# Four DMAs at the head of a bf16 batched matmul: the first a and b loaded in another order

## Chip, core and metric

The kernel runs on one core of a Trainium2 chip, alone on it. The metric is device time in microseconds, the median of repeated executions. One further execution was profiled; its trace gives the time of every instruction and every DMA packet.

## The reference

```python
def reference(a, b):          # a: (16, 512, 512) = (batch, k, m), b: (16, 512, 512) = (batch, k, n), float32
    return np.matmul(a.transpose(0, 2, 1), b).astype(np.float32)
```

Sixteen independent products of 512x512 matrices, with a stored k-first. 33.55 MB are read and 16.78 MB are written, all in float32; the kernel converts to bf16 on the chip and multiplies there.

## The kernel before

**Pairs.** The 16 batches are taken two at a time, so there are eight pairs. A pair's a, and its b, is one SBUF tile of 128 partitions x 8 rows x 512 floats (16 KB in each partition, 2 MB in all). In pairs 1 to 7 the 64 lower partitions hold one batch and the 64 upper ones the other, and one DMA of 2 MB fills the tile. Four such tiles, x0 to x3, are used in turn: a of pair 0 is in x0, b in x1, a of pair 1 in x2, and so on.

**Pair 0 is cut finer.** Its two batches are loaded one after the other, each over all 128 partitions with four rows per partition, so that work can begin after 1 MB of a and 1 MB of b. Batch 0 is cut once more. Of its 512 rows of k, the first 128 go one to a partition (256 KB, one run of 2 KB per partition: `top_v`), and the other 384 go three to a partition (768 KB, one run of 6 KB per partition: `low_v`). Both pieces of a count on one semaphore, `s_f[0]`, both pieces of b on `s_f[1]`; the conversion waits for the full count of 32. Batch 1 of pair 0 follows with one DMA of 1 MB for a and one for b (line 77).

**Engines.** All DMAs are issued by SyncE (SP in the profile) in the order of the program, and all stand in one hardware queue, `q1`, which feeds 16 DMA engines. A load puts eight packets of data on each of the 16 (one per partition) and a four-byte completion packet after them. SP's order is: the four pieces of batch 0 (lines 74 and 75), batch 1 of pair 0 (line 77), fourteen whole tiles (line 83; the last b is cut in two, lines 85 and 86), then the outputs (line 91), the last of them at line 192. From the third pair's a on, a load waits at line 80 until the tile that it overwrites has been converted; the marker for that is the one-element memset of line 102 or 123, which raises `s_in`. The outputs wait for `s_h`, the first half of the last b, at line 88, and for ScalarE's marker `s_out` at line 90: no output is sent before nearly all loads are through.

VectorE (DVE) converts float32 to bf16: lines 98 (pair 0) and 117 (the others), 128x2048 elements at a time. TensorE (PE) multiplies (lines 135 and 155), ScalarE (ACT) copies PSUM to the output tiles (lines 174 and 180). In pair 0 VectorE converts a of batch 0, then b of batch 0, each as soon as its `s_f` is complete; TensorE starts once both are done (line 129).

Of the kernel before, what the change touches and what calls it, by code (L numbers as in the profile page):

```python
# [8 lines left out]
def kernel(  # L9
# [62 lines left out]
    with tc.tile_critical(no_gpsimd_drain=True):  # L72
        for j in range(2):
            nc.sync.dma_start(x_ts[j][:, 0:1, :], top_v[j]).then_inc(s_f[j], 16)  # L74
            nc.sync.dma_start(x_ts[j][:, 1:RV, :], low_v[j]).then_inc(s_f[j], 16)  # L75
        for j in range(2):
            nc.sync.dma_start(x_ts[j][:, RV:R, :], in0_v[j][1]).then_inc(s_x[j], 16)  # L77
# [145 lines left out]
```

## Time and profile before

| | |
|---|---|
| median of 15 runs | 123.64 us (123.28 to 123.96) |
| the profiled execution | 123.85 us, of which 122.1 us are the span from the first to the last instruction |
| DMA packets in the span | 5200, 50.33 MB, 97.6% of 16 engines' time, mean 412 GB/s |
| TensorE matmul / VectorE / ScalarE busy | 62.0 / 38.1 / 32.1 us |
| packets by size | 464 of 4 B, 256 of 2 KB, 256 of 6 KB, 2560 of 8 KB, 1664 of 16 KB |
| typical time of one packet | 84 ns (2 KB), 234 ns (6 KB), 309 ns (8 KB), 611 ns (16 KB) |
| issue of the four pieces of batch 0 | 0.94, 1.39, 1.86 and 2.32 us after the start of the span, each taking 0.39 to 0.43 us of SP |
| from issue to landing of the four | 2.8 us (a, 256 KB), 4.3 us (a, 768 KB), 4.5 us (b, 256 KB), 6.6 us (b, 768 KB) |

The page shares out the span by engine, and the chain of waits says what ended last. A stretch view gives, for a window of time, each engine's busy time and two DMA columns: the share of 16 DMA engines' time, and GB/s. A packet is counted there in the window in which it starts, so in short windows the share can be above 1: packets that began there took longer than the window. The sizes and times of single packets are in the packet records that the trace keeps.

### The profile page before, as it was taken

To read this page: it belongs to the slowest core of one execution; us is meant where nothing else is said; L and a number is where in the kernel's file an instruction comes from. 1 tells how busy PE (TensorE), PEld (TensorE's weight loads), DVE (VectorE), ACT (ScalarE), POOL (GpSimd) and SP (SyncE) were. 2 spreads that over 40 slices of the span, in tenths; PEclk is the share of its full clock that TensorE was granted. 3 is DMA by queue.
4 is the path that set the end of the run, shared out by engine and by line. 5 is a ranking of instruction groups with operands and counts; after the bars stand their busy time and mean duration, and the time that the engine had idled before them with its cause. 6 is when DMAs were issued, how large, how long until landed. Compare 5 with 4: busy or idle time off the path is not lost.

```text
span 122.1 us, 1209 instructions
## 1 busy us (share of the span) xinstructions
PE 62.0 (51%) x480; PEld 35.0 (29%) x480; DVE 38.1 (31%) x48; ACT 32.1 (26%) x41; POOL 0.2 (0%) x4
## 2 busy tenths in 40 slices
PE   0005928379969749979919928989900000000000
PEld 0002404035446324636606605656500000000000
DVE  0133070681394092474356437492000000000000
ACT  4000332400560840091470290091570000000000
POOL 0000000000000000000000000000000000000000
PEclk9999999959999985999999999999997555555555
DMA  3999999999999999999999999999999999999993
GB/s 80 390 419 427 456 435 429 435 435 435 429 429 429 429 429 429 429 429 429 429 429 429 429 429 416 421 427 427 429 429 429 429 427 429 429 429 424 421 427 142
DMA packets 5200, 50.33 MB, mean 412 GB/s; under 512 B 464, under 2 KB 464, under 8 KB 976
## 3 DMA queue, kind: packets, MB, share of 16 engines
q1 hardware_dynamic: 5200, 50.33, 97.6%
HBM read 33.55 MB, written 16.78 MB: 412 GB/s over the span
## 4 chain that ended last, share of the span: by engine, by line
DMA 59%; DVE 6%; issue 3%; ACT 3%; SPq 3%; ACTq 0%
DMA x<-in_b_dram 53%; DMA out_dram<-o 6%; ACT o L180 3%; DVE bbf L117 3%; DVE abf L117 3%; SPq L77 1%; SPq L75 1%; SPq L74 1%; SPq L83 0%; DVE done L123 0%; ACTq L72 0%; SPq L218 0%; SPq L72 0%
## 5 line engine op out<-in xcount | busy, mean ns | idle before, releaser
L155 PE MATMUL ps<-bbf,abf 64*128 64x512 bf16 x448 | 52.9, 393 | 13.2 <-PEq L150 13.2
L155 PEld LDWEIGHTS ps<-bbf,abf 64*128 64x128 bf16 x448 | 31.2, 112 | 34.8 <-issue 20.2
L180 ACT COPY o<-ps 128x1024 f32<-128x1024 f32 x28 | 26.3, 1027 | 40.6 <-PE ps L155 36.5
L117 DVE CAST abf<-x 128x2048 bf16<-128x2048 f32 x14 | 17.1, 1224 | 17.3 <-PE ps L155 13.3
L117 DVE CAST bbf<-x 128x2048 bf16<-128x2048 f32 x14 | 17.2, 1225 | 14.3 <-DMA x<-in_b_dram 14.2
L135 PE MATMUL ps<-bbf,abf 128*128 128x512 bf16 x32 | 9.1, 448 | 13.2 <-PEq L133 13.2
L135 PEld LDWEIGHTS ps<-bbf,abf 128*128 128x128 bf16 x32 | 3.7, 122 | 18.1 <-issue 16.1
L174 ACT COPY o<-ps 128x1024 f32<-128x1024 f32 x4 | 4.1, 1014 | 17.1 <-PE ps L135 17.1
L98 DVE CAST abf<-x 128x2048 bf16<-128x2048 f32 x2 | 2.5, 1226 | 11.5 <-PE ps L135 5.8
L98 DVE CAST bbf<-x 128x2048 bf16<-128x2048 f32 x2 | 2.4, 1224 | 2.0 <-DMA x<-in_b_dram 2.0
L185 ACT ACTIVATE done<-done 1x1 uint32<-1x1 uint32 x8 | 1.6, 197 | 0.0
L174 ACT ACT_TABLE_LOAD x1 | 1.3, 1283 | 0.9 <-SPq L72 0.9
L123 DVE MEMSET done<- 1x1 f32 x14 | 0.8, 59 | 0.0
L102 DVE MEMSET done<- 1x1 f32 x2 | 0.1, 59 | 0.0
L207 POOL MEMSET const-bfloat16-1.0<- 128x1 bf16 x1 | 0.1, 101 | 0.0
L207 POOL MEMSET const-uint8-127<- 128x1 uint8 x1 | 0.1, 101 | 0.0
L207 POOL MEMSET const-float32-0.0<- 128x1 f32 x1 | 0.1, 98 | 0.2 <-issue 0.2
L207 POOL MEMSET const-float32-1.0<- 128x1 f32 x1 | 0.1, 98 | 0.0
## 6 DMA issues: line engine op xcount, KB each, us to landing
out_dram<-o SPq DMA_DIRECT2D x8, 2048.0 KB, 21.8
x<-in_a_dram SPq DMA_DIRECT2D x7, 2048.0 KB, 12.1
x<-in_b_dram SPq DMA_DIRECT2D x6, 2048.0 KB, 15.9
x<-in_b_dram SPq DMA_DIRECT2D x3, 1024.0 KB, 13.5
x<-in_a_dram SPq DMA_DIRECT2D x1, 1024.0 KB, 8.6
x<-in_a_dram SPq DMA_DIRECT2D x1, 768.0 KB, 4.3
x<-in_b_dram SPq DMA_DIRECT2D x1, 768.0 KB, 6.6
x<-in_a_dram SPq DMA_DIRECT2D x1, 256.0 KB, 2.8
```

The lines of the kernel that those rows point to most:

```text
L74: nc.sync.dma_start(x_ts[j][:, 0:1, :], top_v[j]).then_inc(s_f[j], 16)
L75: nc.sync.dma_start(x_ts[j][:, 1:RV, :], low_v[j]).then_inc(s_f[j], 16)
L77: nc.sync.dma_start(x_ts[j][:, RV:R, :], in0_v[j][1]).then_inc(s_x[j], 16)
L98: nc.vector.tensor_copy(out=bf_ts[0][:], in_=x_ts[j][:, u * RV:(u + 1) * RV, :]).then_inc(s_cast, 1)
L117: nc.vector.tensor_copy(out=(bbf_ts if n % 2 else abf_ts)[v][:], in_=x_ts[n % NX][:, v * RV:(v + 1) * RV, :],).then_inc(s_cast, 1)
L123: nc.vector.memset(dve_done[:, n:n + 1], 0.0).then_inc(s_in, 1)
L135: mm = nc.tensor.matmul(ps_ts[0][h][:, t % 2, :], a_m[:, r, t], bbf_ts[0][:, r, :], start=(r == 0), stop=(r == RV - 1),)
L155: mm = nc.tensor.matmul(ps_ts[g][h][:, t % 2, :], a_m[:, t], bbf_ts[v][rows, r, :], start=(v == 0 and r == 0), stop=(v == V - 1 and r == R ...
L174: nc.scalar.copy(out=o_ts[0][:, g, 2 * h:2 * h + 2, :], in_=ps_ts[0][h][:]).then_inc(s_ev[h], 1)
L180: ev = nc.scalar.copy(out=o_ts[i % NO][:, g, 2 * h:2 * h + 2, :], in_=ps_ts[g][h][:])
L185: nc.scalar.memzero(act_done[:, i:i + 1]).then_inc(s_out, 1)
L207: nc = _bacc.Bacc("TRN2", target_bir_lowering=False, num_devices=1)
```

## The change

The four issues of batch 0 come in another order: a's 2 KB runs, b's 2 KB runs, a's 6 KB runs, b's 6 KB runs. Sources, destinations, sizes, semaphores and all waits are the same; no other instruction moves. One line is added to the program, so every line below it has a number higher by one in the kernel after.

```diff
     with tc.tile_critical(no_gpsimd_drain=True):
         for j in range(2):
             nc.sync.dma_start(x_ts[j][:, 0:1, :], top_v[j]).then_inc(s_f[j], 16)
+        for j in range(2):
             nc.sync.dma_start(x_ts[j][:, 1:RV, :], low_v[j]).then_inc(s_f[j], 16)
         for j in range(2):
             nc.sync.dma_start(x_ts[j][:, RV:R, :], in0_v[j][1]).then_inc(s_x[j], 16)
```

## Prediction

> **What bounds the kernel now.** I read the page's second and third parts first.
>
> ```profile
> DMA  3999999999999999999999999999999999999993
> GB/s 80 390 419 427 456 435 429 435 435 435 429 429 429 429 429 429 429 429 429 429 429 429 429 429 416 421 427 427 429 429 429 429 427 429 429 429 424 421 427 142
> q1 hardware_dynamic: 5200, 50.33, 97.6%
> ```
>
> The 16 DMA engines are full from the first slice to the last; TensorE, the busiest compute engine, has 51%. The time is one stream of 50.33 MB plus what stands before and behind it. An instruction in pair 0 matters only if it opens a gap in that stream, or makes one engine later than the rest. So I looked at both ends of the stream with the stretch view (its last two columns: share of the DMA engines, GB/s).
>
> ```profile
> 0.90:1.80 0.90, 0.00 (x0) 0.00 (x0) 0.00 (x0) 0.90 (x1) 0.00 (x0) 1.00 0.00 0
> 1.80:2.40 0.60, 0.00 (x0) 0.00 (x0) 0.00 (x0) 0.38 (x1) 0.00 (x0) 1.00 1.00 109
> 2.40:3.00 0.60, 0.00 (x0) 0.00 (x0) 0.00 (x0) 0.00 (x0) 0.00 (x0) 1.00 0.65 253
> 3.40:5.00 1.60, 0.00 (x0) 0.00 (x0) 0.00 (x0) 0.00 (x0) 0.00 (x0) 1.00 1.02 419
> 5.40:5.60 0.20, 0.00 (x0) 0.00 (x0) 0.00 (x0) 0.00 (x0) 0.00 (x0) 1.00 1.08 389
> 5.60:5.90 0.30, 0.00 (x0) 0.00 (x0) 0.21 (x1) 0.00 (x0) 0.00 (x0) 1.00 1.83 499
> 5.90:8.60 2.70, 0.00 (x0) 0.00 (x0) 1.01 (x1) 0.00 (x0) 0.00 (x0) 1.00 0.96 402
> 119.90:120.30 0.40, 0.00 (x0) 0.00 (x0) 0.00 (x0) 0.00 (x0) 0.00 (x0) 0.50 0.36 144
> 120.30:120.90 0.60, 0.00 (x0) 0.00 (x0) 0.00 (x0) 0.00 (x0) 0.00 (x0) 0.50 0.07 27
> ```
>
> Data start about 1.96 us (packet records), 1.0 us after the first issue. By 3.00 us 0.6 x 109 + 0.6 x 253 = 217 KB are through, so a's 256 KB end near 3.1. The row 5.40:5.60 holds 2 KB packets alone: 389 GB/s, so a 256 KB piece is 262 KB / 389 = 0.67 us. The row 3.40:5.00 holds 6 KB packets: 419 GB/s, so a 768 KB piece is 786 KB / 419 = 1.88 us.
>
> Two rows matter more than the rates. In 5.60:5.90, where b's 6 KB runs begin, 499 x 0.3 = 150 KB were started; at 26.2 GB/s per engine (419 / 16) that is 5.7 engine-us of work, but 1.83 x 0.3 x 16 = 8.8 were recorded: some 3 engine-us of stall. The packet records give its shape: two 6 KB packets took 1.09 us in place of 0.234, five took 0.45 to 0.52. At the other such place, a's first 6 KB runs at about 3.05, eight packets took 0.39 to 0.64. Then the end: in 120.30:120.90 the share is 0.07, and 27 x 0.6 = 16 KB, two packets of 8 KB. So two engines finish about half a microsecond after the other fourteen. A stall of 0.86 us on two engines at 5.9 us can live to the end, because each engine has its own fixed share of every transfer and never idles; completion packets fit this, since in the later transfers two of 16 always land some 0.5 us late.
>
> The ends add up: 1.96 us to the first byte, 118.85 of stream (to 120.81), 1.30 to the end of the span, 1.75 outside it (123.85 less 122.1). The median, 123.64, is 0.21 below this execution; I make the sum against 123.85 and carry the difference to the median.
>
> VectorE's rows show the cover on the compute side, SP's the issues:
>
> ```profile
> 0.94 0.39 SPq L74 DMA_DIRECT2D x<-in_a_dram  x1
> 1.39 0.42 SPq L75 DMA_DIRECT2D x<-in_a_dram  x1
> 1.86 0.42 SPq L74 DMA_DIRECT2D x<-in_b_dram  x1
> 2.32 0.43 SPq L75 DMA_DIRECT2D x<-in_b_dram  x1
> 5.68 1.23 DVE L98 CAST abf<-x 128x2048 bf16<-128x2048 f32 x1 [5.68 <-DMA x<-in_a_dram]
> 8.95 1.23 DVE L98 CAST bbf<-x 128x2048 bf16<-128x2048 f32 x1 [2.04 <-DMA x<-in_b_dram]
> ```
>
> **What the skill says.** The Trainium skill, "DMA: Bandwidth & Descriptors", section "Queues, rings and completion order": each DMA engine consumes one queue's descriptors in ring order. The trace agrees: 6 KB packets begin only when the 2 KB ones are through. Its section "Where 436 GB/s comes from" puts the fabric's ceiling at 435 GB/s; the page's long plateau is 429. "HBM Reference", section "Latency", gives an HBM access 0.2 us on average and 2 us under high load: the stalls of 0.16 to 0.86 us lie in that span, though the trace doesn't show that they are read latency.
>
> **The change part by part.** Nothing is removed or added. a's 768 KB issue moves behind b's 256 KB issue on SP: it starts at 1.86 in place of 1.39, b's small one at 1.39 in place of 1.86. Each still takes 0.39 to 0.43 us of SP, and everything from 2.32 on keeps its time.
>
> *Does the queue run dry?* First data came 1.0 us after issue, so the second transfer is ready at 2.4 and needed at 3.1 (0.7 spare); a's large one is ready at 2.9 and needed at 3.1 + 0.67 = 3.8 (0.9 spare); b's large one is ready at 3.3 and needed at 3.8 + 1.88 = 5.7. Cost 0. Were that cover gone, the gap would go straight into the time.
>
> *When do the tiles land?* a gets b's 256 KB ahead of it: its conversion moves from 5.68 to 6.35 and ends at 7.58. Behind it on VectorE is b's conversion, which waits for data until 8.95, with the same bytes ahead of it as before; 1.37 us spare, so TensorE still starts at 10.5. Cost 0. Even a TensorE start later by a microsecond would be harmless: the first load that waits for VectorE is issued at 17.29, while the loads ahead of it land only at 23.6 (the last of them was issued at 4.29 and took 19.3 us).
>
> *What happens to the stalls?* This is the only term that can show. Both groups stood at a change from 2 KB to 6 KB packets; at 6 to 8 KB there is none above 0.05 us, at 6 to 2 KB one of 0.17. Before there are two such changes; after there is one, and one place where a 2 KB transfer follows a 2 KB transfer, which the trace of before doesn't contain. Lower bound: the long stalls don't occur, the two late engines end with the rest, -0.5 us. Upper bound: a second stall of the long kind on an engine that has one already, +0.86. I take 0: a stall follows each short transfer (0.67 us gives little time to fetch what comes next), and there are two short transfers in either order.
>
> Sum: 123.85 + 0 + 0 + 0, carried to the median 123.64; I write 123.65. A difference under 0.2%, 0.25 us, is about what can't be told from no change.
>
> **The rivals.**
>
> *Slower: the stalls pile up.* After the change both exposed places lie back to back at 3.1 and 3.8 us, with no long transfer between them in which an engine's reads could run ahead again. If one engine has the 0.4 us kind at the first and the 0.86 kind at the second, and an engine decides the end that had only one before, the time is +0.3 to +0.6: 124.1. It decides when the slowest engine's stalls exceed 0.86 by 0.25. For it: eight of 16 engines stalled at the first place already. Against it: of the two engines with the long stall one seems to have had 0.30 at the first place too, and the other none, so the sum of both was partly there before.
>
> *Faster: the long stall is a matter of b's 6 KB runs following its 2 KB runs.* With a's 1.88 us between them it goes; the last two packets end with the rest, and 0.5 us is saved: 123.1. For it: the long stall stood there alone. Against it: a's large piece now starts after a 2 KB transfer and a full stream, just as b's did.
>
> *The change doesn't reach the time in any way but a conversion of a later by 0.67 us.* This is the forecast itself: the order of four pieces within the first 2 MB, hidden behind the wait for the second of them.
>
> **How the numbers follow.** Same 0.40 (123.65, own range 123.4 to 123.9), slower 0.36 (at 124.1, reaching 124.5 at the bound), faster 0.24 (at 123.1). I lean to slower over faster because two short transfers in a row are the one condition that is new, and a new exposed place costs more easily than it gives. The range that leaves about 2 in 10 outside is 123.1 to 124.25.
>
> **What would show it.** Right: issues in the new order at the same four times; a's first conversion near 6.35, b's near 8.95, TensorE at 10.5; stalled packets at about 3.1 and 3.8, none at 5.7; two packets alone at the end near 120.8. b's conversion at 8.4, and no lone packets at the end, would be the faster rival; b's conversion past 9.2 with every later load late by the same amount the slower one. The reasoning itself is wrong if the DMA share drops below full in 2.4 to 4 us (the queue ran dry), or if the time moves by more than the lateness of the slowest engine does.

## The result and the profile after

The kernel after takes 125.62 us (median of 9, 125.0 to 126.25) against 123.58 us for the kernel before on the same chips (median of 47). The ratio is 1.0163, 95% interval 1.0148 to 1.0178. The prediction was 123.65 us, no change, with a range of 123.1 to 124.25 us; the measured time lies above it.

The page of the kernel after, DMA rows of its second and third part:

```profile
DMA  2999999999999999999999999979999999999992
GB/s 69 375 405 423 454 427 422 438 427 427 380 396 448 427 443 427 427 427 433 422 427 448 427 438 409 419 309 406 422 435 427 435 427 427 422 422 435 425 438 108
q1 hardware_dynamic: 5200, 50.33, 96.0%
```

Same packets, same bytes, but 96.0% of the engines' time in place of 97.6%, in a span of 124.2 us in place of 122.1. The plateau is the same; there are dents at the start, in slices 11 and 12 (380 and 396 GB/s, from 31.0 to 37.3 us), and in slice 27 (309 GB/s). The span has grown by 2.1 us, and the profiled execution by as much (125.99 against 123.85).

The timeline of the kernel after (start, length, instruction; in brackets the idle time before and what ended it):

```profile
0.94 0.39 SPq L74 DMA_DIRECT2D x<-in_a_dram  x1
1.39 0.42 SPq L74 DMA_DIRECT2D x<-in_b_dram  x1
1.86 0.42 SPq L76 DMA_DIRECT2D x<-in_a_dram  x1
2.33 0.43 SPq L76 DMA_DIRECT2D x<-in_b_dram  x1
...
4.22 1.41 SPq L84 DMA_DIRECT2D x<-in_b_dram  x1
8.87 1.23 DVE L99 CAST abf<-x 128x2048 bf16<-128x2048 f32 x1 [8.87 <-DMA x<-in_a_dram]
10.72 1.23 DVE L99 CAST bbf<-x 128x2048 bf16<-128x2048 f32 x1 [0.62 <-DMA x<-in_b_dram]
```

The issues came in the new order at the foreseen times. a's conversion, foreseen at 6.35 us, starts at 8.87; b's, foreseen at 8.95, at 10.72. One issue, the eighth, held SP for 1.41 us in place of 0.45; the trace doesn't show why. The stretch view (last two columns: share of the 16 DMA engines, GB/s) shows what happened in between:

```profile
2.40:3.40 1.00, 0.00 (x0) 0.00 (x0) 0.00 (x0) 0.00 (x0) 0.00 (x0) 1.00 0.89 326
3.90:4.80 0.90, 0.00 (x0) 0.00 (x0) 0.00 (x0) 0.00 (x0) 0.00 (x0) 1.00 0.90 373
4.80:5.70 0.90, 0.00 (x0) 0.00 (x0) 0.00 (x0) 0.00 (x0) 0.00 (x0) 1.00 0.87 362
5.70:6.30 0.60, 0.00 (x0) 0.00 (x0) 0.00 (x0) 0.00 (x0) 0.00 (x0) 1.00 0.78 318
6.30:7.50 1.20, 0.00 (x0) 0.00 (x0) 0.00 (x0) 0.00 (x0) 0.00 (x0) 1.00 1.06 410
81.00:82.50 1.50, 1.50 (x18) 0.89 (x14) 1.41 (x2) 0.00 (x0) 0.00 (x0) 1.00 0.42 175
122.40:123.00 0.60, 0.00 (x0) 0.00 (x0) 0.00 (x0) 0.00 (x0) 0.00 (x0) 0.50 0.07 27
```

The same stretches of the kernel before, for comparison:

```profile
3.90:4.80 0.90, 0.00 (x0) 0.00 (x0) 0.00 (x0) 0.00 (x0) 0.00 (x0) 1.00 1.02 423
5.70:6.30 0.60, 0.00 (x0) 0.00 (x0) 0.60 (x1) 0.00 (x0) 0.00 (x0) 1.00 1.18 376
81.00:82.50 1.50, 1.36 (x14) 0.94 (x16) 1.50 (x3) 1.50 (x2) 0.00 (x0) 1.00 1.01 426
```

From 3.9 to 5.7 us a share of 0.87 to 0.90 is 14 of 16 engines. The packet records say the same: two engines had finished b's 2 KB runs at 3.9 us and got their first packet of a's 6 KB runs only at 6.3 to 6.5 us, at least 4.4 us after that transfer's issue. On the other engines it was there when it was needed, from 3.81 us on, so after 1.95 us or little more. Between 5.8 and 6.2 us two more engines stood still, at the change to the fourth transfer. Of the sixteen completions of a's 768 KB, fourteen come at 6.01 to 6.34 us and two at 8.68 and 8.84; a's conversion waits for all sixteen. The two stay behind: in 122.40:123.00 there are again two packets alone (27 x 0.6 = 16 KB).

How the 2.14 us between the two profiled executions (125.99 less 123.85) come together can be read from the last completion of one and the same transfer. For a's 1 MB of batch 1 it stands at 13.17 us, before at 11.38: 1.8 us later. In the kernel before, too, two engines were late by then, by some 0.6 us; the pair's longer hole makes most of the 1.8. First data at 2.32 us in place of 1.96 goes into the same sum, but in this execution alone: in the next profile of this kernel they come at 1.96, and the time is no shorter. The 1.8 us still stand at 30 us (30.21 against 28.42). By 50 us they have become 2.2 (50.03 against 47.87), and so they stay to the end.

The last 0.4 us come in at a later hole, between 32 and 36 us:

```profile
29.95 0.33 SPq L84 DMA_DIRECT2D x<-in_a_dram  x1
32.00:34.00 2.00, 2.00 (x22) 1.29 (x19) 1.23 (x1) 0.00 (x0) 0.00 (x0) 1.00 0.93 336
```

The same two in the kernel before:

```profile
26.00 0.33 SPq L83 DMA_DIRECT2D x<-in_a_dram  x1
32.00:34.00 2.00, 1.58 (x16) 0.65 (x12) 0.74 (x1) 2.00 (x3) 0.00 (x0) 1.00 1.05 451
```

With both conversions late, TensorE starts at 12.24 us in place of 10.48, takes 5.18 us for its second batch in place of 3.62, and VectorE reaches the next pair at 26.40 in place of 22.33. So this load, the eleventh transfer, is issued only at 29.95 us in place of 26.00. The first engines need it at 32.09. Three engines then stand still; their first packets come between 32.7 and 33.4 us, up to 3.5 us after the issue. The late pair has work there, but its packets, like the others', are longer while the stream recovers (up to 0.93 us in place of 0.61, at 34 to 35 us). That this hole is what costs the pair 0.4 us is read from the time alone: in the next profile, with the same load issued at 30.81 us, the last engines lose nothing there.

The row 81.00:82.50 is one more hole, in the other fourteen engines. SP waits at line 89 for the first half of the last b before it sends outputs, and that is complete only when the late pair is; the timely engines have nothing left by then.

### The profile page after: what moved, and what is told of

It is laid out like the page before. It is cut to its first block, busy times and chain, and to the rows that moved or that the text cites. A ratio compares the mean times of both kernels' runs of the same rounds, so it can differ in the third digit from the quotient of the medians.

```text
span 124.2 us, 1209 instructions
## 1 busy us (share of the span) xinstructions
PE 62.7 (50%) x480; PEld 35.0 (28%) x480; DVE 37.9 (30%) x48; ACT 32.1 (26%) x41; POOL 0.2 (0%) x4
## 2 busy tenths in 40 slices
DMA packets 5200, 50.33 MB, mean 405 GB/s; under 512 B 464, under 2 KB 464, under 8 KB 976
## 3 DMA queue, kind: packets, MB, share of 16 engines
q1 hardware_dynamic: 5200, 50.33, 96.0%
## 5 line engine op out<-in xcount | busy, mean ns | idle before, releaser
L156 PE MATMUL ps<-bbf,abf 64*128 64x512 bf16 x448 | 51.3, 385 | 14.4 <-PEq L151 14.4
L136 PE MATMUL ps<-bbf,abf 128*128 128x512 bf16 x32 | 11.4, 534 | 15.0 <-PEq L134 15.0
```

The source lines that it names most:

```text
L136: mm = nc.tensor.matmul(ps_ts[0][h][:, t % 2, :], a_m[:, r, t], bbf_ts[0][:, r, :], start=(r == 0), stop=(r == RV - 1),)
L156: mm = nc.tensor.matmul(ps_ts[g][h][:, t % 2, :], a_m[:, t], bbf_ts[v][rows, r, :], start=(v == 0 and r == 0), stop=(v == V - 1 and r == R ...
```

## Experiments

**Is it a fixture of each order?** Both kernels were profiled once more.

> The kernel before, profiled once more, to see whether the late pair of DMA engines is a fixture of this order. Theory P (the late pair sets the end, and it is made late in the first 8 us by a fixed cause): again a stall near 5.9 us on two engines, about 0.9 us each, again two completions of 16 that land some 0.5 us after the rest in every later transfer, time 123.3 to 123.9. Rival R (the stalls are chance): another number of engines, another place, or none.

123.68 us, in one execution. Of the kernel before again, stretch view:

```profile
3.90:4.80 0.90, 0.00 (x0) 0.00 (x0) 0.00 (x0) 0.00 (x0) 0.00 (x0) 1.00 1.05 437
4.80:5.70 0.90, 0.00 (x0) 0.00 (x0) 0.00 (x0) 0.00 (x0) 0.00 (x0) 1.00 0.91 357
5.70:6.30 0.60, 0.00 (x0) 0.00 (x0) 0.45 (x1) 0.00 (x0) 0.00 (x0) 1.00 1.00 341
```

This time four to five engines stood still between 5.8 and 6.3 us, where b's 6 KB runs, the fourth transfer, are due; the lateness is spread over more engines. At 3.9 to 4.8 us nearly all were busy (1.05). In these two executions the place is the same and the number of engines is not: theory P in its strict form (always a pair) fell.

> The kernel after, profiled once more. In its first profile two engines did nothing between 3.9 and 6.3 us: they had finished b's 2 KB runs and had no packet of a's 6 KB runs. Theory P: the same hole of 2.0 to 2.6 us on two engines, a's landing near 8.8 us, time 125 to 126.3. Rival R: the hole moves or is missing in this execution, and the time with it.

126.39 us, in one execution. Of the kernel after again:

```profile
3.90:4.80 0.90, 0.00 (x0) 0.00 (x0) 0.00 (x0) 0.00 (x0) 0.00 (x0) 1.00 0.81 253
4.80:5.70 0.90, 0.00 (x0) 0.00 (x0) 0.00 (x0) 0.00 (x0) 0.00 (x0) 1.00 0.72 266
5.70:6.30 0.60, 0.00 (x0) 0.00 (x0) 0.00 (x0) 0.00 (x0) 0.00 (x0) 1.00 0.90 297
```

253 GB/s in place of 423: eight engines stood still at 3.75 to 4.5 us, three of them past 6 us (their completions of a come at 9.3, the first at 6.0). In both profiles of this kernel the hole begins as soon as the second transfer is through; the number of engines and the width differ.

**Which of the two holes costs?**

```diff
-        nc.sync.wait_ge(s_h, 16)
         for i in range(pairs - 1):
             nc.sync.wait_ge(s_out, i + 1)
```

> The kernel after without SP's wait for the first half of the last b ahead of the outputs. After the change this wait let the 14 timely engines run dry from 81.0 to 82.6 us (0.86 us of 16 engines' time). Theory P (the end is set by the two late engines, which never run dry after 6.3 us): the gap closes, the 14 others end earlier, and the time stays at 125.6 within 0.3. Rival G (the loss is this gap): about 0.9 us comes back, 124.7.

125.19 us, ratio 1.0145 (1.0104 to 1.0186). Of this kernel:

```profile
3.90:4.80 0.90, 0.00 (x0) 0.00 (x0) 0.00 (x0) 0.00 (x0) 0.00 (x0) 1.00 0.45 137
...
81.00:82.50 1.50, 1.15 (x13) 0.52 (x10) 1.42 (x2) 1.50 (x3) 0.00 (x0) 1.00 1.00 421
```

The gap at 81 us is closed (421 GB/s), and 1.45% of the 1.63% remain. By these ratios a ninth of the loss is the wait ahead of the outputs; the intervals overlap and allow anything from nothing to a third. The time lies between the two forecasts, nearer to theory P's. Most of the loss is thus made earlier; in this execution ten engines stood still after 3.7 us.

**Do the later issues crowd out the third transfer?** The 256 KB pieces got semaphores of their own, `s_t`, VectorE waits for them as well, and SP waits before the fifth issue (only this line is shown, with the two lines behind it):

```diff
+        nc.sync.wait_ge(s_t[0], 16)
         for j in range(2):
             nc.sync.dma_start(x_ts[j][:, RV:R, :], in0_v[j][1]).then_inc(s_x[j], 16)
```

> The kernel after, with SP waiting for the landing of a's 256 KB (near 3.8 us) before it issues the fifth transfer and all later ones; the 256 KB pieces get semaphores of their own for that. Theory S (what the two engines lack is the third transfer's work, which reaches them late because the two transfers ahead of it are short; later issues have no part in it): the hole of 2.4 us stays, 125.6. Rival Q (the fifth to eighth issue, which crowd behind it between 2.8 and 5.6 us, hold it up): the hole shrinks below 1 us, and the time goes to 124.2 or less.

Median 125.99 us over 20 runs, 1.9% above the kernel before (123.64). They scatter from 123.43 to 126.90, and 18 of the 20 took 124.89 us or more. The ratio on record, 1.006 (1.0021 to 1.01), is drawn from the quickest few and says little here. The hole is there while only the fourth transfer stands behind the third: SP issues the fifth at 3.69 us, when the first engines are already running dry.

```profile
3.90:4.80 0.90, 0.00 (x0) 0.00 (x0) 0.00 (x0) 0.00 (x0) 0.00 (x0) 1.00 0.33 116
4.80:5.70 0.90, 0.00 (x0) 0.00 (x0) 0.00 (x0) 0.00 (x0) 0.00 (x0) 1.00 0.88 266
```

Rival Q is out: the hole did not shrink. Two of the runs came in at 123.4. That fits a delay that differs from execution to execution, with the third transfer sometimes in time; it isn't shown, as those two runs weren't profiled.

**How much must stand ahead of the third transfer?** Three forms, their first four issues made by SP at the same times. The lines that differ are shown, without the lines that they replace:

```diff
# whole: one DMA of 1 MB each, 8 KB runs
+            nc.sync.dma_start(x_ts[j][:, 0:RV, :], in0_v[j][0]).then_inc(s_f[j], 16)
# 4 KB runs: four pieces of 512 KB
+    top_v = [x[0][0:2 * P].rearrange("(p r) m -> p r m", r=2) for x in (a, b)]
# 6 KB first
         for j in range(2):
             nc.sync.dma_start(x_ts[j][:, 1:RV, :], low_v[j]).then_inc(s_f[j], 16)
         for j in range(2):
             nc.sync.dma_start(x_ts[j][:, 0:1, :], top_v[j]).then_inc(s_f[j], 16)
```

> a and b of batch 0 are each one DMA of 1 MB with 8 KB runs; no 256 KB pieces. Theory S (the third transfer's work reaches a DMA engine only some 3 to 4.5 us after its issue once the stream runs, at 4.8 to 6.3 us of the span, and an engine that is through with the first two transfers before that stands still): the third transfer is needed only at 2 + 2 x 2.5 = 7 us, so no engine stands still, no late engine at the end, 122.9 to 123.5, no slower than the kernel before. Rival K (two transfers of the same size in a row are what stalls, whatever the size): engines stand still near 4.5 or 7 us, 124.5 or more.

> The order of the kernel after, but each of the four pieces is 512 KB with 4 KB runs. Theory S: the third transfer is needed at about 2 + 2 x 1.25 + 0.3 = 4.8 us, in the midst of its arrival times of 4.8 to 6.3: fewer engines stand still, the last two or three of them up to 1.5 us in place of 2.4; the time lies between both kernels, 124.0 to 125.0. Rival P (only what follows a packet of 2 KB stalls): no engine stands still, 123.5 or less.

> The same four pieces with the two of 768 KB first: a's 6 KB runs, b's 6 KB runs, a's 2 KB runs, b's 2 KB runs. Theory S: the third is needed at 2 + 2 x 1.88 + 0.2 = 6.0 us, the fourth at 6.6, the fifth at 7.3: nearly all has arrived, no hole over 0.5 us, 123.2 to 123.8. Rival P (what follows 2 KB packets stalls): two short transfers in a row as in the kernel after, so engines stand still at 7.3 us, 125 or more.

| first two transfers | first engine through with both, us | measured, us | ratio to before (95%) |
|---|---|---|---|
| 2 x 256 KB (kernel after) | 3.8 | 125.62 | 1.0163 (1.0148 to 1.0178) |
| 2 x 512 KB (4 KB runs) | 4.9 | 124.05 (123.09 to 124.57) | 1.0022 (1.0000 to 1.0043) |
| 256 + 768 KB (kernel before) | 5.0 | 123.64 | 1 |
| 2 x 768 KB (6 KB first) | 6.3 | 123.48 | 0.9987 (0.9978 to 0.9995) |
| 2 x 1 MB (whole) | 7.4 | 123.21 (123.13 to 123.39) | 0.9963 (0.9951 to 0.9976) |

The medians fall with each step, though between 4 KB runs and the kernel before the interval reaches 1. The cleanest pair is the kernel after and 6 KB first: the same four pieces in another order, and 125.62 against 123.48 us. Three stretch views (4 KB runs, 6 KB first, whole, in this order):

```profile
4.80:5.70 0.90, 0.00 (x0) 0.00 (x0) 0.00 (x0) 0.00 (x0) 0.00 (x0) 1.00 0.98 319
```

```profile
4.80:5.70 0.90, 0.00 (x0) 0.00 (x0) 0.00 (x0) 0.00 (x0) 0.00 (x0) 1.00 0.96 389
5.70:6.30 0.60, 0.00 (x0) 0.00 (x0) 0.00 (x0) 0.00 (x0) 0.00 (x0) 1.00 1.07 451
6.30:7.50 1.20, 0.00 (x0) 0.00 (x0) 0.00 (x0) 0.00 (x0) 0.00 (x0) 1.00 0.98 379
```

```profile
4.80:5.70 0.90, 0.00 (x0) 0.00 (x0) 0.00 (x0) 0.00 (x0) 0.00 (x0) 1.00 1.00 419
5.70:6.30 0.60, 0.00 (x0) 0.00 (x0) 0.49 (x1) 0.00 (x0) 0.00 (x0) 1.00 1.00 423
6.30:7.50 1.20, 0.00 (x0) 0.00 (x0) 0.74 (x1) 0.00 (x0) 0.00 (x0) 1.00 1.02 430
```

With 4 KB runs there is still a dent, 319 GB/s; eleven completions of the third transfer come by 6.65 us, the other five 0.3 to 1.5 us later. With 6 KB first, two transfers of 2 KB packets in a row stand at 6.3 to 7.5 us and run at their usual rate. Rivals K and P are out: neither two equal transfers in a row nor what follows 2 KB packets stalls. The whole form beats both kernels: no engine is late at the end, and 0.43 us is saved. Not all of that is lateness. Summed over the packet records its packets took 1893 us of engine time, those of the kernel before 1903: 0.6 us less for each of 16 engines. In the 6 KB order a's conversion starts at 7.74 us, 2.06 later than before, at no cost; but b's, for which TensorE waits as well, starts at 8.88 (8.95 before). The cover that this shows is a's behind b's, and no more.

**Is it the time of the issue?**

```diff
-            nc.sync.dma_start(x_ts[j][:, 1:RV, :], low_v[j]).then_inc(s_f[j], 16)
+            nc.scalar.dma_start(x_ts[j][:, 1:RV, :], low_v[j]).then_inc(s_f[j], 16)
```

> The kernel after with the two 768 KB pieces issued by ScalarE, ahead of its table load, on a queue of its own, so that all four pieces are issued by 1.9 us, before data flow; packets of both queues then take turns. Theory S (an issue that comes before the stream runs arrives within 1.0 us, a later one needs 3 to 4.5): every engine has work from 2 us on, and no engine stands still for more than 0.5 us up to about 7 us, 123.7 or less. Rival B (two engines are hampered at 4 to 6.3 us by something else than the time of the issue): the hole of two or more engines stays, 125 or more.

123.28 us, ratio 0.9965 (0.9950 to 0.9980). The timeline of this kernel; all four issues begin by 1.39 us:

```profile
0.90 0.40 ACTq L76 DMA_DIRECT2D x<-in_a_dram  x1
0.94 0.39 SPq L74 DMA_DIRECT2D x<-in_a_dram  x1
1.33 0.45 ACTq L76 DMA_DIRECT2D x<-in_b_dram  x1
1.39 0.42 SPq L74 DMA_DIRECT2D x<-in_b_dram  x1
```

Its stretch view has 428 GB/s at 3.9 to 4.8 us and 392 at 4.8 to 5.7; no engine stands still. But two things changed, the time of the issue and the queue. So the same with ScalarE held back by a semaphore until SP has issued its two pieces (the lines added to the run with two queues, without the declaration of the semaphore):

```diff
+        nc.sync.sem_inc(s_go, 1)
+        nc.scalar.wait_ge(s_go, 1)
```

> The run with two queues again, but ScalarE issues the two 768 KB pieces only after SP has issued both of 256 KB, at about the same 1.86 and 2.3 us as in the kernel after; SP goes on with its fifth transfer at the same time. Theory S (what counts is that the issue comes before the stream runs): engines that are through with 512 KB at 3.8 us stand still again, several of them, and the time is 124.3 or more. Rival N (what helped was the queue of its own, not the early issue): no engine stands still, as when issued at 0.90 and 1.33 us, 123.3.

130.39 us, ratio 1.0513 (1.0466 to 1.0561). Of this kernel:

```profile
3.90:4.80 0.90, 0.00 (x0) 0.00 (x0) 0.00 (x0) 0.20 (x1) 0.00 (x0) 1.00 0.64 184
...
25.00:28.20 3.20, 1.08 (x6) 0.34 (x3) 2.08 (x3) 1.36 (x2) 0.00 (x0) 1.00 0.00 0
```

Eight to nine engines stand still at 3.75 to 5.2 us: a queue of its own doesn't help a transfer that is issued at 1.89 us. Its first packet on any engine comes at 4.71 us. The size of the loss has another cause. Packets of both queues took turns, b of batch 0 was complete only at 19.2 us, and the next load, which waits for a later conversion, was issued only at 27.40 us. All engines stood still for 3 us at 25 to 28. Its 130 us are not the price of the first hole.

Last, the third issue was held back in one queue. The 256 KB pieces count on the semaphores `s_t` again, as in the run that held the fifth issue:

```diff
+        nc.sync.wait_ge(s_t[0], 16)
         for j in range(2):
             nc.sync.dma_start(x_ts[j][:, 1:RV, :], low_v[j]).then_inc(s_f[j], 16)
```

> The kernel after, with SP waiting for the landing of a's 256 KB (near 3.7 us) before it issues the third transfer: that issue moves from 1.86 to about 3.75 us, when most engines have run dry. Theory S in its first form (an issue needs 1.0 us to reach the engines when they are idle, 3 to 4.5 when they stream): the third arrives on all engines near 4.8 to 5.2 us, no engine stands still up to 6.3, and although it is issued 1.9 us later the time is no worse than the kernel after, 124.6 to 125.6. Rival F (a fixed delay of 3 to 4.5 us from the issue for every transfer behind the second): the third arrives between 6.8 and 8.2, the hole grows by the 1.9 us, 127 or more.

125.15 us, ratio 1.0138 (1.0106 to 1.0171). Timeline and stretch view of this kernel:

```profile
3.66 0.33 SPq L78 DMA_DIRECT2D x<-in_a_dram  x1
```

```profile
3.40:3.90 0.50, 0.00 (x0) 0.00 (x0) 0.00 (x0) 0.00 (x0) 0.00 (x0) 1.00 0.58 221
3.90:4.80 0.90, 0.00 (x0) 0.00 (x0) 0.00 (x0) 0.00 (x0) 0.00 (x0) 1.00 0.38 55
5.70:6.30 0.60, 0.00 (x0) 0.00 (x0) 0.00 (x0) 0.00 (x0) 0.00 (x0) 1.00 1.01 420
```

Issued 1.8 us later, the third transfer reaches the first engine at 4.61 us and the last at about 5.1: 0.95 to 1.5 us after its issue, in place of up to 4.4. All engines are empty for a moment, all are served at nearly one time, and by 5.7 the stream is whole (420 GB/s), earlier than in the kernel after. The time is still 1.4% longer than before, as all sixteen engines now lose some: none had a packet from 3.95 to 4.6 us, and the first packets took up to 1.12 us in place of 0.234. Rival F, a fixed delay from the issue, is out.

## Why the prediction was wrong

*What bounds the kernel; the ends of the stream.* Right. The stream of 50.33 MB set the time in both kernels, and the lateness of the slowest engines at 6 us was still there at the end.

*"Does the queue run dry?"* This step failed, and with it the sum: its 0 was nearly all of the 2 us. It took the 1.0 us from the first issue to the first data as the time that every issue needs, and so gave a's large piece 0.9 us to spare. That 1.0 us was measured on idle engines. Behind a running stream the runs show, on the late engines, at least 4.4 us from issue to first packet (after), 2.9 to 3.2 for most of them in the run without SP's wait, and 0.95 to 1.5 again on idle engines (late issue). First packets at 4.8 to 6.5 us against a need at 3.8 (3.6 without SP's wait) make the hole. The prediction named this very case as its check ("the queue ran dry") but gave it no rival and no chance.

*"What happens to the stalls?"* The stalls were seen, but put down to the change from short to long packets, and that isn't it: in the 6 KB order no engine stands still behind the 2 KB packets. In the second profile of the kernel before, engines had no packet at all at this place until 6.2 to 6.4 us: the fourth transfer, issued at 2.32, was needed at 5.7 and was late there. It is likely that the two packets of 1.09 us at 5.9 us in the first profile are the same lateness; it isn't shown, as there the packets had begun. (The records have four packets of 0.45 to 0.52 us beside them, not five.) The order after brings the need forward: issued at the same 1.86 us, the third transfer was needed at 5.0 before and at 3.8 after.

*"When do the tiles land?"* The landings were wrong with the hole (8.87 in place of 6.35, 10.72 in place of 8.95). That a's conversion may come later as long as b's does not held in the 6 KB order. The ample cover behind a later start of TensorE was not there: the prediction looked at the first load that waits for VectorE, but with TensorE 1.8 us late the load two further on, at 29.95 us, came too late for three engines. With two late queues the gap is 3 us, at 25 to 28 us.

*The rivals.* "Slower: the stalls pile up" had the sign, and the place (back-to-back transfers at 3.1 and 3.8 us), but not the mechanism or the size: 124.1 against 125.62. "Faster" was the wrong order for its right observation: what removes the late engines is more work ahead of the third transfer, or an earlier issue of it.

The Trainium skill, "DMA: Bandwidth & Descriptors", section "Why a DMA increments its semaphore by 16 and not by 1", says that a transfer's engines finish independently and that only the full count means that all has landed. The runs agree: fourteen completions at 6.34 us or before, two at 8.68 and 8.84, and a conversion that starts at 8.87.

What stays open: why an issue behind a running stream arrives late, and why on some engines and not on others. The trace shows when packets start, not how the work reached the engine. That it is the running stream rests in the first microseconds on the late-issue run alone, and there another reading fits: its data came at 4.6 to 5.1 us, which is also when most late engines of other runs got theirs, so a hindrance that ends at a fixed time after the start would do as well. Places far from the start speak against that. In the run with two late queues a load is issued at 27.40 us to engines that are all idle; on fifteen of them its first packets start 1.0 to 1.6 us later, on the last 2.3. In the kernel after, the first output is issued at 81.65 us while fourteen engines run dry, and starts on them 0.9 to 1.1 us later. The load issued there at 29.95 us behind a full stream needed up to 3.5 us. No run was made to separate the two readings.

## What to carry to other kernels

At the head of a stream, count for each transfer the time from its issue to the moment when the engines are through with what stands ahead of it, and measure the issue-to-data time under load, not on the first transfer: here about 1.0 us on idle engines, and up to 4.4 us or more behind a stream. Here two transfers of 256 KB at the head gave too little cover; two of 768 KB, or the first four issued from two engines before any data flowed, gave enough. With their issues about a microsecond later, the two queues were the slowest form of all. A DMA engine that falls behind by microseconds early on can stay behind to the end, so look at the spread of the completions within one transfer, not only at the last of them.

## What was not expected

The prediction had nothing of either of these; the expectations of the runs did. The fewest pieces won: without the 256 KB pieces, which let data start in smaller portions, batch 0's a is converted at 5.81 us (5.68 before) and b at 8.24 (8.95 before), and the time is 123.21 us. And an issue held back by 1.8 us had all of a on the chip earlier than one that wasn't: a's conversion starts at 7.81 us in place of 8.87.
